# Temporaries of the next stage's right operands held once, and the first half's norm sums behind the third product, in a two-layer streaming encoder step

## The chip, the cores and the metric

The kernel runs on one core of one Trainium2 chip. The metric is the device time of one execution in microseconds. Engines are named as in the profile: PE (TensorE, the matrix products; PEld is its loading of weights), DVE (VectorE), ACT (ScalarE), POOL (GpSimd) and SP (SyncE, which issues most loads). L451 means line 451 of the kernel before. An order of instructions or a row of the profile that names a tile as `fr<-W` reads: tile fr is written from W.

## The reference

Two layers, each a mixer (gated linear attention, then latent attention) between two half-step SwiGLU feed-forward blocks, for 512 new frames, 32 frames of a running stream and 16 meta tokens, which makes T = 560 columns. All of it is float32. The change is in the feed-forward blocks (FFN):

```python
def rmsnorm(x, w):
    x32 = x.astype(jnp.float32)
    y = x32 * lax.rsqrt(jnp.mean(x32 * x32, axis=-1, keepdims=True) + RMS_EPS)
    return (y * w.astype(jnp.float32)).astype(x.dtype)

def swiglu_half(h, norm_w, w_gate, w_up, w_down):
    hn = rmsnorm(h, norm_w)
    return h + 0.5 * ((jax.nn.silu(hn @ w_gate) * (hn @ w_up)) @ w_down)
...
    for i in range(DEPTH):
        hp = swiglu_half(hp, ffn1_norm[i], ffn1_w_gate[i], ffn1_w_up[i], ffn1_w_down[i])
...
        hp = swiglu_half(hp, ffn2_norm[i], ffn2_w_gate[i], ffn2_w_up[i], ffn2_w_down[i])
```

The model width is 1024, the width of the FFN 2816. The same weights serve both groups of frames.

## The kernel before

**Precision.** Each float32 operand is split into a high part (an ACT cast, L331) and a low part (a DVE subtraction, L332). A product is three matmuls per 128 rows: high by high (L378), low weight by high (L379), high weight by low (L381). Of weights the two parts are called whi and wlo, of activations ah and al, and of right operands both are x.

**Gate and up products.** Both are computed by Strassen's scheme: seven products of quadrants in place of eight, each of 24 matmuls with 272 or 280 columns, into the PSUM tiles A, B and C. For each pair of 128-row tiles of the FFN, `gate_up` runs through them in this order, named by their right operands: b11 (into A), b21 (C), t6 (A), t5 (B), t7 (A), t4 (C), b22 (B). `quads` supplies the left operands: it loads the quadrants r11, r12, r21 and r22 of the weights into tiles fr (256 KB a load, two loads a quadrant, six tiles in turn) and forms four sums on DVE (L451), s1 = r21 + r22, r21 + r11, r11 + s1 and r12 + r11. The sum r11 + s1 is the left operand of t6, s1 that of t5, r21 + r11 that of t7. Each is then cast and split. The first two left operands of an FFN are loaded and cast ahead of it (`first_weights`).

**Right operands.** For all FFNs but the first, the right operands of the seven products are made while the stage before still runs: whenever its last loop has finished a piece of the stream h (one of eight row tiles m, one of two column halves hf), `Quads.__call__` makes the parts for it. Its temporaries b12, t5, q (four 280-column parts) and sq2 (the squares for the norm) come from the pool xt. The first FFN makes its right operands itself (`lazy`).

**Norm.** The norm's scale is applied to the results of the products and not to their operands. `Net.roots` makes it for one column half: PE adds the squares over the rows (L410, three matmuls of one column), DVE takes the inverse root in 11 small operations (L424 to L432), PE spreads it over the rows (L417, three transposes), and ACT copies it (L272). `finish` then combines the products (L497, L499), multiplies by the scale (L501), applies SiLU and the product of gate and up (L504), and splits the result into ah and al.

**Stages.** ffn(1,0) = f1_0, the first mixer, ffn(2,0) = f2_0, ffn(1,1) = f1_1, the second mixer, ffn(2,1) = f2_1. The row tiles of the FFN are handled in five groups; the down products of a group (tiles Y, weights raw, one load of 512 KB a row tile) fill gaps between products of the next group, and those of the last group form a loop of 16 pieces, in whose course the next stage's right operands are made. Where f2_0 and f2_1 begin, that loop is the mixer's output product (tiles ps), of 16 pieces too.

**Order.** The program is written stage by stage; the compiler's scheduler then sets the order on each engine by its own model of readiness. Each engine and each queue works strictly in its order. Loads go through SP's queue. A tile of a pool is an address in SBUF; a write to it waits until the last reader of whatever lay at that address is done, also if that was a tile of another pool. In f2_0 and f1_1 the pool xt lies, in the kernel before, at 148704 to 166624 bytes of each partition, and overlaps the end of the six fr tiles (125056 to 149632); in f2_1 it lies at 151936 to 169856, and its second q overlaps the first fr tile (168928 to 173024).

Of the kernel before, what the change touches and what calls it, by code (L numbers as in the profile page):

```python
# [10 lines left out]
F32 = mybir.dt.float32  # L11
# [7 lines left out]
P = 128  # L19
# [3 lines left out]
T = SEQ + LS + META  # L23
# [72 lines left out]
class Normed(list):  # L96
# [7 lines left out]
    def parts(self, m, hf):  # L104
        net, nc = self.net, self.net.nc
        c = slice(*self.halves[hf])
        if not self:
            self.extend((net.xtile(), net.xtile()) for _ in range(ND))
            self.y = net.np_.tile([P, T], F32, name="yn", tag="yn")
        hm, w = net.h[:, m, c], net.nv[:, self.w0 + m:self.w0 + m + 1]  # L110
        hi, lo = self[m]
        nc.scalar.activation(hi[:, c], hm, AF.Copy, scale=w)
        nc.vector.scalar_tensor_tensor(lo[:, c], hm, w, hi[:, c].bitcast(F32), op0=ALU.mult, op1=ALU.subtract)

    def square(self, hf):
        c0, c1 = self.halves[hf]
        m = self.squared[hf]
        self.net.square(self.net.h[:, m, c0:c1], c1 - c0, hf, m == 0)
        self.squared[hf] += 1
# [15 lines left out]
class Quads(Normed):  # L135
# [51 lines left out]
    def parts(self, m, hf):  # L187
        net, nc, n = self.net, self.net.nc, self.n
        v = nc.vector
        i = m % 4  # L190
        if hf == 0:
            self.scaled_parts("b11" if m < 4 else "b21", i, m)
        elif m < 4:
            b12, t5 = (self.tmp.tile([P, 280], F32, name=x, tag=x, bufs=2)[:, :n] for x in ("b12", "t5"))
            nc.scalar.activation(b12, self.piece(m, 1), AF.Copy, scale=self.weight(m))
            v.scalar_tensor_tensor(t5, self.piece(m, 0), self.weight(m), b12, op0=ALU.mult, op1=ALU.subtract)
            net.split(*self.place("t5", i), t5)
            self.kept[i] = b12, t5
        else:
            b12, t5 = self.kept.pop(i)  # L200
            q = self.tmp.tile([P, 4, 280], F32, name="q", tag="q", bufs=2)
            t6, b22, t7, t4 = (q[:, j, :n] for j in range(4))
            nc.scalar.activation(b22, self.piece(m, 1), AF.Copy, scale=self.weight(m))
            v.scalar_tensor_tensor(t6, t5, -1.0, b22, op0=ALU.mult, op1=ALU.subtract)
            v.tensor_tensor(t7, b22, b12, op=ALU.subtract)
            v.scalar_tensor_tensor(t4, self.piece(m, 0), self.weight(m), t6, op0=ALU.mult, op1=ALU.add)
            self.place("t6", i)
            t = self.sets["t6"][1][i]
            net.split(t[:, 0, :, :n], t[:, 1, :, :n], q[:, :, :n])

    def square(self, m):

        net, nc = self.net, self.net.nc
        c1 = self.halves[1][1]
        sq = self.tmp.tile([P, T], F32, name="sq2", tag="sq2", bufs=2)
        nc.scalar.activation(sq[:, :c1], net.h[:, m, :c1], AF.Square)
        for hf, (a, b) in enumerate(self.halves):
            if m == 0:
                net.accs[hf] = net.np_.tile([P, 280], F32, name="acc", tag="acc")
                nc.vector.tensor_copy(net.accs[hf][:, :b - a], sq[:, a:b])  # L220
            else:
                acc = net.accs[hf][:, :b - a]
                nc.vector.tensor_tensor(acc, acc, sq[:, a:b], op=ALU.add)
# [66 lines left out]
class Net:  # L290
# [176 lines left out]
    def gate_up(self, i, l, f, xs, act, raws, tp, between):  # L467


        nc = self.nc  # L470
        v = nc.vector
        n = xs.n
        left = self.quads(i, l, f, raws, xs.early, xs.left)
        done = []

        def product(to, op, more=False):
            if xs.lazy and op in ("b11", "b21"):
                w, x = next(left), xs.operand(op)
            else:
                x, w = xs.operand(op), next(left)  # L480
            for j in range(2):
                self.mm(to[:, j, :n], w, 4 * j, x, (0, n), more)

        def gap():
            done.append(0)
            between(len(done))

        def copy(of, tag):
            r = tp.tile([P, 2, 280], F32, name="r", tag=tag, bufs=1)
            nc.scalar.copy(r[:, :, :n], of[:, :, :n])  # L490
            return r

        def finish(j, hf, bank, r, how):
            gu = tp.tile([P, 2, 280], F32, name="gu", tag="gu", bufs=2)
            b, r, t = bank[:, :, :n], r[:, :, :n], gu[:, :, :n]
            if how == "neg":
                v.scalar_tensor_tensor(t, b, -1.0, r, op0=ALU.mult, op1=ALU.subtract)  # L497
            else:
                v.tensor_tensor(t, b, r, op=how)  # L499
            y = xs.scale(hf).unsqueeze(1).to_broadcast([P, 2, n])  # L500
            v.tensor_tensor(t, t, y, op=ALU.mult)  # L501
            g, u = gu[:, 0, :n], gu[:, 1, :n]
            nc.scalar.activation(g, g, AF.Silu)
            v.tensor_tensor(g, g, u, op=ALU.mult)  # L504
            c = slice(*xs.halves[hf])
            self.split(act[j][0][:, c], act[j][1][:, c], g)

        first = not xs.finish
        A = self.bank2("A")
        product(A, "b11")  # L510
        r1 = copy(A, "ra")
        gap()
        C = self.bank2("C")
        product(C, "b21")
        if not first:
            finish(0, 0, C, r1, ALU.add)
        gap()
        if first and not xs.lazy:
            xs.roots(0)
        product(A, "t6", True)  # L520
        r2 = copy(A, "rb")
        gap()
        if first and xs.lazy:
            xs.roots(0)
        B = self.bank2("B")
        product(B, "t5")
        p5 = copy(B, "rc")
        if first:
            finish(0, 0, C, r1, ALU.add)
            xs.roots(1)  # L530
        gap()
        product(A, "t7", True)
        r3 = copy(A, "ra")
        finish(1, 1, A, p5, "neg")
        gap()
        D = self.bank2("C")
        product(D, "t4")
        finish(1, 0, D, r3, ALU.subtract)
        gap()
        product(B, "b22", True)  # L540
        finish(0, 1, B, r2, ALU.add)
        gap()
# [373 lines left out]
    def softmax(self, pool, p, parts):  # L916

        nc = self.nc
        st = pool.tile([P, 8], F32, name="st", tag="st", bufs=4)
        for i, (s, n, c) in enumerate(parts):  # L920
            nc.vector.reduce_max(st[:, i:i + 1], s[:, :n], axis=AX.X)
        if len(parts) == 2:
            nc.vector.tensor_tensor(st[:, 0:1], st[:, 0:1], st[:, 1:2], op=ALU.max)
        nc.vector.tensor_scalar(st[:, 2:3], st[:, 0:1], -SCALE, None, op0=ALU.mult)
        for i, (s, n, c) in enumerate(parts):
            nc.scalar.activation(p[:, c:c + n], s[:, :n], AF.Exp, bias=st[:, 2:3], scale=SCALE,
                                 accum_out=st[:, 3 + i:4 + i])
        if len(parts) == 2:
            nc.vector.tensor_tensor(st[:, 3:4], st[:, 3:4], st[:, 4:5], op=ALU.add)
        nc.vector.reciprocal(st[:, 5:6], st[:, 3:4])  # L930
        n = sum(q[1] for q in parts)
        nc.vector.tensor_scalar(p[:, :n], p[:, :n], st[:, 5:6], None, op0=ALU.mult)
# [637 lines left out]
```

## Time and profile before

| | |
|---|---|
| median of 3 runs | 2114.17 us (2113.75 to 2114.99) |
| the profiled execution | 2109.41 us, of which 2107.5 are its span |
| mean granted clock of TensorE | 0.982 |
| PE busy | 2026.0 us, 96% of the span |
| DVE busy | 1643.2 us, 78% |
| ACT busy | 1018.4 us, 48% |
| POOL busy | 51.4 us, 2% |
| loads from HBM | 176.84 MB, 86 GB/s over the span |

The profile records one execution. The busy share of an engine is an average over all stages. A row of the timeline has the start in us, the duration in us, the engine, the line, the operation with its output and inputs, a count and, in brackets, how long the engine stood idle ahead of it and which operation ended that. The chain that ended last is followed back from the last instruction, at each step to what released it. The clock is what the throttle granted TensorE, 1.00 being full speed.

### The profile page before, as it was taken

What the parts mean: (1) busy time and instruction counts of PE and PEld (TensorE: products, weight loads), DVE (VectorE), ACT (ScalarE), POOL (GpSimd) and SP (SyncE); (2) the same over time, 40 slices, a digit from 0 to 9 for tenths busy, and PEclk for the clock granted to TensorE, in tenths of its full rate; (3) what the DMA queues carried; (4) which work ended last, traced back from release to release, by engine and by line L of the source; (5) the groups of instructions that cost most, each with busy time, mean ns of one, the idle gap of its engine ahead of it and who ended that gap; (6) DMA issues with size and microseconds to landing.
All of it is one profiled execution on the core that took longest, in us unless ns stands there. A gap on an engine that the chain in (4) does not pass through costs nothing.

```text
span 2107.5 us, 38039 instructions
## 1 busy us (share of the span) xinstructions
PE 2026.0 (96%) x15290; PEld 1980.2 (94%) x15290; DVE 1643.2 (78%) x3097; ACT 1018.4 (48%) x1822; POOL 51.4 (2%) x117
## 2 busy tenths in 40 slices
PE   5999999999999899999989999999999979999997
PEld 5999999989999799999979999999988969999997
DVE  8887878556658888788778877886788788878884
ACT  6444445455445444445545444454575454444451
POOL 0000000101110000000000000000210000000000
PEclk8999999999999899999989999999999989999998
DMA  3323222222221332322222322222211223232221
GB/s 131 106 87 107 93 96 78 77 68 71 73 80 55 108 103 82 106 86 91 81 95 96 105 92 91 95 83 92 61 51 59 71 86 100 90 111 91 96 72 62
DMA packets 93633, 183.29 MB, mean 87 GB/s; under 512 B 10433, under 2 KB 22081, under 8 KB 93457
## 3 DMA queue, kind: packets, MB, share of 16 engines
q1 hardware_dynamic: 89632, 176.24, 26.1%
q10 hardware_dynamic: 3824, 4.63, 0.7%
q8 instruction: 120, 1.97, 0.4%
q14 instruction: 57, 0.46, 0.1%
HBM read 176.84 MB, written 3.99 MB: 86 GB/s over the span
## 4 chain that ended last, share of the span: by engine, by line
PE 82%; DVE 10%; ACT 3%; DMA 2%; issue 2%; SPq 0%; POOL 0%; DVEq 0%; ACTq 0%; POOLq 0%
PE Y L381 8%; PE Y L378 8%; PE Y L379 8%; PE A L379 5%; PE A L381 5%; PE A L378 5%; PE ps L378 4%; PE ps L381 4%; PE ps L379 4%; PE B L378 3%; PE B L379 3%; PE B L381 3%; PE C L379 3%; PE C L381 3%; PE C L378 3%; DVE wlo L332 3%
## 5 line engine op out<-in xcount | busy, mean ns | idle before, releaser
L332 DVE TENSOR_TENSOR wlo<-fr,whi 128x1024 fp32r<-128x1024 f32 x302 | 363.9, 1216 | 17.2 <-ACT whi L331 17.0
L378 PE MATMUL Y<-ah,whi 128*128 128x280 f32 (+1 forms) x1408 | 373.8, 291 | 1.9 <-ACT ah L331 1.0
L379 PE MATMUL Y<-ah,wlo 128*128 128x280 f32 (+1 forms) x1408 | 373.4, 292 | 0.0
L331 ACT CAST whi<-fr 128x1024 fp32r<-128x1024 f32 x302 | 313.3, 1049 | 92.9 <-PE C L381 34.6
L378 PE MATMUL A<-x,whi 128*128 128x280 f32 (+1 forms) x1056 | 286.3, 296 | 29.5 <-ACT whi L331 29.5
L379 PE MATMUL A<-x,wlo 128*128 128x280 f32 (+1 forms) x1056 | 285.7, 296 | 1.0 <-DVE wlo L332 1.0
L378 PEld LDWEIGHTS Y<-ah,whi 128*128 128x128 f32 x1408 | 265.2, 188 | 3.4 <-ACT ah L331 1.7
L556 DVE SCALAR_TENSOR_TENSOR h<-Y,h 128x280 f32<-128x280 f32 (+1 forms) x320 | 140.9, 443 | 161.9 <-PE Y L381 161.2
L379 PEld LDWEIGHTS Y<-ah,wlo 128*128 128x128 f32 x1408 | 265.4, 188 | 0.0
L332 DVE TENSOR_TENSOR wlo<-raw,whi 128x512 fp32r<-128x512 f32 (+5 forms) x237 | 203.6, 861 | 76.7 <-ACT whi L331 71.9
L331 ACT CAST whi<-raw 128x512 fp32r<-128x512 f32 (+5 forms) x237 | 176.0, 744 | 173.4 <-PE ps L381 55.2
L381 PE MATMUL Y<-al,whi 128*128 128x280 f32 (+1 forms) x1408 | 233.9, 292 | 0.0
L378 PEld LDWEIGHTS A<-x,whi 128*128 128x128 f32 x1056 | 203.9, 193 | 31.1 <-ACT whi L331 31.1
L451 DVE TENSOR_TENSOR fr<-fr 128x1024 f32<-128x1024 f32 x176 | 214.5, 1219 | 20.4 <-DMA fr<-W 18.1
L379 PEld LDWEIGHTS A<-x,wlo 128*128 128x128 f32 x1056 | 203.7, 193 | 1.7 <-DVE wlo L332 1.4
L381 PEld LDWEIGHTS Y<-al,whi 128*128 128x128 f32 x1408 | 201.2, 189 | 0.0
L378 PE MATMUL B<-x,whi 128*128 128x280 f32 (+1 forms) x704 | 188.6, 293 | 3.4 <-ACT whi L331 3.4
L379 PE MATMUL C<-x,wlo 128*128 128x280 f32 (+1 forms) x704 | 187.1, 292 | 3.5 <-DVE wlo L332 3.5
L379 PE MATMUL B<-x,wlo 128*128 128x280 f32 (+1 forms) x704 | 187.4, 292 | 0.8 <-DVE wlo L332 0.8
L378 PE MATMUL C<-x,whi 128*128 128x280 f32 (+1 forms) x704 | 187.4, 291 | 0.6 <-ACT whi L331 0.6
L381 PE MATMUL A<-x,whi 128*128 128x280 f32 (+1 forms) x1056 | 181.2, 294 | 0.0
L490 ACT COPY r<-A 128x560 f32<-128x560 f32 (+1 forms) x132 | 82.2, 623 | 174.1 <-PE A L381 173.8
(368 smaller groups left out, 4059.2 us busy)
## 6 DMA issues: line engine op xcount, KB each, us to landing
fr<-W SPq DMA_DIRECT2D x352, 256.0 KB, 3.4
raw<-W SPq DMA_DIRECT2D x80, 512.0 KB, 3.5
raw<-W SPq DMA_DIRECT2D x112, 256.0 KB, 2.9
raw<-W SPq DMA_DIRECT2D x40, 128.0 KB, 2.1
h<-xT SPq DMA_DIRECT2D x3, 560.0 KB, 7.6
raw<-W SPq DMA_DIRECT2D x4, 384.0 KB, 3.1
o_y<-h SPq DMA_DIRECT2D x8, 136.0 KB, 2.2
o_y<-h ACTq DMA_DIRECT2D x8, 136.0 KB, 1.9
```

The costliest lines, as they stand in the source:

```text
L331: self.nc.scalar.copy(hi, src)
L332: self.nc.vector.tensor_tensor(lo, src, hi.bitcast(F32), op=ALU.subtract)
L378: f(hi[:, b0 + k, :], xh[:, c], start=not more and k == 0, stop=False)
L379: f(lo[:, b0 + k, :], xh[:, c], start=False, stop=False)
L381: f(hi[:, b0 + k, :], xl[:, c], start=False, stop=k == n - 1)
L451: add = lambda out, x, y: nc.vector.tensor_tensor(out, x, y, op=ALU.add)
L490: nc.scalar.copy(r[:, :, :n], of[:, :, :n])
L556: nc.vector.scalar_tensor_tensor(self.h[:, m, c], Y[:, :n], 0.5, self.h[:, m, c], op0=ALU.mult, op1=ALU.add)
```

## The change

The temporaries b12, t5, q and sq2 are held in one buffer each in place of two, which makes the pool xt 8960 bytes a partition in place of 17920. With it its address moves: to 157664 to 166624 in f2_0 and f1_1 (over the second gu tile only), and to 151936 to 160896 in f2_1 (its q now over the tile ra, the copy of the first product, and no fr tile). And `gate_up` asks for the first half's norm sums behind the third product (t6) for every FFN, which only the lazy first one did.

```diff
--- before.py
+++ after.py
@@ -191,14 +191,14 @@
         if hf == 0:
             self.scaled_parts("b11" if m < 4 else "b21", i, m)
         elif m < 4:
-            b12, t5 = (self.tmp.tile([P, 280], F32, name=x, tag=x, bufs=2)[:, :n] for x in ("b12", "t5"))
+            b12, t5 = (self.tmp.tile([P, 280], F32, name=x, tag=x, bufs=1)[:, :n] for x in ("b12", "t5"))
             nc.scalar.activation(b12, self.piece(m, 1), AF.Copy, scale=self.weight(m))
             v.scalar_tensor_tensor(t5, self.piece(m, 0), self.weight(m), b12, op0=ALU.mult, op1=ALU.subtract)
             net.split(*self.place("t5", i), t5)
             self.kept[i] = b12, t5
         else:
             b12, t5 = self.kept.pop(i)
-            q = self.tmp.tile([P, 4, 280], F32, name="q", tag="q", bufs=2)
+            q = self.tmp.tile([P, 4, 280], F32, name="q", tag="q", bufs=1)
             t6, b22, t7, t4 = (q[:, j, :n] for j in range(4))
             nc.scalar.activation(b22, self.piece(m, 1), AF.Copy, scale=self.weight(m))
             v.scalar_tensor_tensor(t6, t5, -1.0, b22, op0=ALU.mult, op1=ALU.subtract)
@@ -212,7 +212,7 @@
 
         net, nc = self.net, self.net.nc
         c1 = self.halves[1][1]
-        sq = self.tmp.tile([P, T], F32, name="sq2", tag="sq2", bufs=2)
+        sq = self.tmp.tile([P, T], F32, name="sq2", tag="sq2", bufs=1)
         nc.scalar.activation(sq[:, :c1], net.h[:, m, :c1], AF.Square)
         for hf, (a, b) in enumerate(self.halves):
             if m == 0:
@@ -515,12 +515,10 @@
         if not first:
             finish(0, 0, C, r1, ALU.add)
         gap()
-        if first and not xs.lazy:
-            xs.roots(0)
         product(A, "t6", True)
         r2 = copy(A, "rb")
         gap()
-        if first and xs.lazy:
+        if first:
             xs.roots(0)
         B = self.bank2("B")
         product(B, "t5")
```

What stands in a row on the engines follows from the scheduler. PE at the start of f2_0, before (C is the second product, A the third, t6, and B the fourth, t5; ry is the inverse root):

```order
L381 MATMUL C_8011<-x_7603,whi_7780 128x280
L381 MATMUL C_8011<-x_7604,whi_7780 128x280
L410 MATMUL Y_8036<-ones_67,acc_7660 128x1 x3
L417 MATMUL Y_8127<-ident_66,ry_8040 128x128 x3
L410 MATMUL Y_8137<-ones_67,acc_7662 128x1 x3
L417 MATMUL Y_8187<-ident_66,ry_8141 128x128 x3
L378 MATMUL A_7978<-x_7609,whi_8064 128x280
L378 MATMUL B_8094<-x_7605,whi_8095 128x280
L379 MATMUL A_7978<-x_7609,wlo_8065 128x280
L378 MATMUL A_7978<-x_7610,whi_8064 128x280
```

The same place after:

```order
L381 MATMUL C_8011<-x_7603,whi_7780 128x280
L381 MATMUL C_8011<-x_7604,whi_7780 128x280
L410 MATMUL Y_8076<-ones_67,acc_7660 128x1 x3
L378 MATMUL A_7978<-x_7609,whi_8046 128x280
L378 MATMUL B_8094<-x_7605,whi_8095 128x280
L379 MATMUL A_7978<-x_7609,wlo_8047 128x280
L378 MATMUL A_7978<-x_7610,whi_8046 128x280
L379 MATMUL A_7978<-x_7610,wlo_8047 128x280
```

and 40 rows on, at the end of B:

```order
L381 MATMUL B_8094<-x_7607,whi_8095 128x280
L381 MATMUL B_8094<-x_7608,whi_8095 128x280
L417 MATMUL Y_8127<-ident_66,ry_8080 128x128 x3
L410 MATMUL Y_8137<-ones_67,acc_7662 128x1 x3
L378 MATMUL A_7978<-x_7609,whi_8155 128x280
L379 MATMUL A_7978<-x_7609,wlo_8156 128x280
L378 MATMUL A_7978<-x_7610,whi_8155 128x280
```

The sums of the first half (L410) stay ahead of A; the transposes (L417) and the second half's sums move behind B. f2_1 is alike; in f1_1 the fourth product, B, begins ahead of the third.

DVE at the start of f2_0, before, the end of the second chain of roots and the four sums of quadrants:

```order
L504 TENSOR_TENSOR gu_8125<-gu_8125 128x280
L431 TENSOR_TENSOR rt_8143<-rt_8143,rv_8142 128x3
L432 SCALAR_TENSOR_TENSOR ry_8141<-rt_8143,ry_8141 128x3
L430 TENSOR_TENSOR rt_8143<-ry_8141 128x3
L431 TENSOR_TENSOR rt_8143<-rt_8143,rv_8142 128x3
L332 TENSOR_TENSOR al0_7975<-gu_8125,ah0_7974 128x280
L432 SCALAR_TENSOR_TENSOR ry_8141<-rt_8143,ry_8141 128x3
L451 TENSOR_TENSOR fr_8060<-fr_8054,fr_8057 128x1024
L451 TENSOR_TENSOR fr_8054<-fr_8054,fr_7979 128x1024
L451 TENSOR_TENSOR fr_7979<-fr_7979,fr_8060 128x1024
L451 TENSOR_TENSOR fr_7982<-fr_7982,fr_7979 128x1024
L332 TENSOR_TENSOR wlo_8065<-fr_7979,whi_8064 128x1024
```

and after:

```order
L499 TENSOR_TENSOR gu_8125<-C_8011,r_8009 128x560
L451 TENSOR_TENSOR fr_8042<-fr_8036,fr_8039 128x1024
L424 TENSOR_SCALAR rv_8081<-Y_8076 128x3
L451 TENSOR_TENSOR fr_8036<-fr_8036,fr_7979 128x1024
L425 TENSOR_SCALAR ry_8080<-rv_8081 128x3
L451 TENSOR_TENSOR fr_7979<-fr_7979,fr_8042 128x1024
L430 TENSOR_TENSOR rt_8082<-ry_8080 128x3
L451 TENSOR_TENSOR fr_7982<-fr_7982,fr_7979 128x1024
L332 TENSOR_TENSOR wlo_8047<-fr_7979,whi_8046 128x1024
L431 TENSOR_TENSOR rt_8082<-rt_8082,rv_8081 128x3
L332 TENSOR_TENSOR wlo_8096<-fr_8042,whi_8095 128x1024
L432 SCALAR_TENSOR_TENSOR ry_8080<-rt_8082,ry_8080 128x3
```

The four sums now follow the first result (L499) directly, and the small operations of the roots stand between sums and casts. f2_1 is alike.

SP in the last down loop of f2_0, ahead of f1_1 (raw_11996 to raw_12326 are down weights and the first two left operands; fr_12449 to fr_12748 belong to f1_1), before:

```order
L358 DMA fr_11654<-W 128x512 x2
L341 DMA raw_11996<-W 128x1024
L341 DMA raw_12030<-W 128x1024
L341 DMA raw_12137<-W 128x1024
L341 DMA raw_12171<-W 128x1024
L358 DMA raw_12278<-W 128x512 x2
L358 DMA raw_12285<-W 128x512 x2
L341 DMA raw_12292<-W 128x1024
L341 DMA raw_12326<-W 128x1024
L341 DMA raw_12820<-W 128x256
L341 DMA raw_12882<-W 128x256
```

and after:

```order
L358 DMA fr_11654<-W 128x512 x2
L358 DMA fr_12449<-W 128x512 x2
L358 DMA fr_12452<-W 128x512 x2
L341 DMA raw_11996<-W 128x1024
L358 DMA fr_12506<-W 128x512 x2
L358 DMA fr_12509<-W 128x512
L341 DMA raw_12030<-W 128x1024
L358 DMA fr_12509<-W 128x512
L341 DMA raw_12137<-W 128x1024
L358 DMA fr_12748<-W 128x512 x2
L341 DMA raw_12171<-W 128x1024
L358 DMA raw_12278<-W 128x512 x2
```

The first ten loads of f1_1's quadrants moved from behind the last of the down weights to between them; the casts of its third and fourth left operands moved into the end of this loop too. In f2_1 the place of the loads on SP is the same, directly behind raw_20697; what they wait for is not: before, the first of them waits for the reader of the second q, and after only for tiles of the mixer. In f2_0 they stand where they stood, and wait for the mixer's last output product as before.

## Prediction

> **What bounds the kernel now.** I read the page first: busy shares, the chain that ended last, then the costliest groups with the idle time before them.
>
> ```profile
> span 2107.5 us, 38039 instructions
> ...
> PE 82%; DVE 10%; ACT 3%; DMA 2%; issue 2%; SPq 0%; POOL 0%; DVEq 0%; ACTq 0%; POOLq 0%
> ...
> L378 PE MATMUL A<-x,whi 128*128 128x280 f32 (+1 forms) x1056 | 286.3, 296 | 29.5 <-ACT whi L331 29.5
> ...
> L490 ACT COPY r<-A 128x560 f32<-128x560 f32 (+1 forms) x132 | 82.2, 623 | 174.1 <-PE A L381 173.8
> ```
>
> The kernel is bound by PE, so time is only to be had where PE stands still. The largest single wait is in the third row: product A waits for a cast weight, 29.5 us in all. At the three starts that the diff touches it is 3.76, 3.76 and 6.17 in the rows below, 13.7 of the 29.5. (The last row is used further down.) I then read those three starts in the timeline, PE alone. Stage f2_0 (start, length, what, idle time before it and releaser):
>
> ```profile
> 685.12 0.72 PE L410 MATMUL Y<-ones,acc 128*128 128x1 f32 x6
> ...
> 693.59 0.87 PE L417 MATMUL Y<-ident,ry 128*128 128x128 f32 x3 [3.30 <-DVE ry L432]
> 698.23 0.60 PE L378 MATMUL A<-x,whi 128*128 128x280 f32 x1 [3.76 <-ACT whi L331]
> 699.18 0.60 PE L378 MATMUL B<-x,whi 128*128 128x280 f32 x1 [0.35 <-ACT whi L331]
> 699.58 0.57 PE L379 MATMUL A<-x,wlo 128*128 128x280 f32 x1
> ...
> 707.05 0.29 PE L378 MATMUL A<-x,whi 128*128 128x280 f32 x1
> 707.18 0.29 PE L379 MATMUL A<-x,wlo 128*128 128x280 f32 x1
> ```
>
> The second product (C) ends where L410 begins, at 685.1; the fifth (t7) begins at 707.05. Between them lie two products of 24 matmuls, which at full clock start 0.13 us apart (the last two rows; 0.129 over a product, 3.1 us). So 21.9 us are spent on 6.2 us of products. What ends the idle time is the chain of waits, same stage:
>
> ```profile
> 685.90 0.73 DVE gu L499
> ...
> 693.45 1.15 DVE fr L451
> 694.61 1.24 DVE fr L451
> 695.87 1.24 DVE fr L451
> 697.24 0.84 issue
> 698.08 1.05 ACT whi L331
> ```
>
> DVE's sums of weight quadrants (L451) begin only after both root chains, because they stand behind them on DVE; from the first sum (693.4) to the first A is 4.8 us, and to the second matmul of A (699.58) 6.1. What else could hold the sums is their data. Loads in 682 to 692 us, and the rate at which the DMA engines moved them:
>
> ```profile
> fr<-W SPq DMA_DIRECT2D x4, 256.0 KB, 6.3
> ```
>
> ```profile
> 685.00:688.00 3.00, 0.85 (x9) 0.76 (x7) 2.76 (x10) 0.16 (x1) 0.00 (x0) 1.00 1.02 374
> ```
>
> 256 KB at 374 GB/s are 0.70 us, and loads queue. The last half of quadrant r22, issued near 682.3, lands at about 688.6.
>
> **The change, part by part.** It adds and takes away no arithmetic: the same sums, casts, products and loads, in another order and other buffers.
>
> *f2_0.* The loads still wait for the last matmul of the mixer's output (same buffers' owner), so they land when they did. The order now has L410 of the first half, then A and B, and DVE's four sums ahead of the root chain. The first sum starts at 688.7 (landing; L499 has ended by 686.6), 4.7 us before 693.4; first A at 693.5, its second matmul at 694.8, and 0.3 later for the small root operations that now stand between the sums: 695.1. Off that gain come the clock and the roots. Busy time in windows of 3.41 us, where the eighth column is the granted clock (columns: length, then busy us and count of PE, PEld, DVE, ACT, POOL, then clock, DMA share, GB/s):
>
> ```profile
> 685.79:689.20 3.41, 0.53 (x6) 0.47 (x5) 2.53 (x13) 0.00 (x0) 0.00 (x0) 1.00 0.89 341
> 689.20:692.61 3.41, 1.09 (x7) 1.01 (x5) 2.10 (x10) 1.05 (x3) 0.00 (x0) 0.50 0.00 2
> ...
> 699.44:702.85 3.41, 3.41 (x15) 3.33 (x16) 3.41 (x4) 1.58 (x2) 0.00 (x0) 0.50 0.59 181
> 702.85:706.26 3.41, 3.41 (x28) 3.41 (x27) 0.41 (x2) 1.57 (x2) 0.00 (x0) 1.00 0.85 274
> ```
>
> After a window with little PE work the clock is 0.50, and it is back one window after a full one; a full window holds 15 matmuls at half clock (0.23 us each), so half clock costs 0.10 us a matmul. PE still has nothing to do from 685.9 to 693.5, so the drop stays. If the windows keep their phase, matmuls run slowly from 695.1 to 699.44, 19 matmuls in place of 14: 0.5 us more. The 46 matmuls left after the opening end at 699.44 + 27 x 0.129 = 703.0. Then the first half's L417 x3 and the second half's L410 x3, which used to run in idle time, now stand in PE's stream (about 0.4 + 0.36 from their spacing): t7 begins at 703.8 in place of 707.05, 3.25 us earlier. The second L417 x3 (0.4) now stands inside the next block's first product, and waits for a chain of 11 small DVE operations which stand between casts; I allow 0.5 for that. Net 2.3; ends 0 (sums no earlier than L499 plus a full chain, phase unlucky: +1.5) and 3.5 (no wait, lucky phase). I take 2.2.
>
> [...]
>
> *f1_1.* This is where most of it lies. Here the new, smaller temporaries leave the weight buffers untouched (only the second gu buffer is overlapped), and the order moves the weight loads, the four sums and the casts into the last down phase of the FFN before.
>
> ```profile
> 1077.00 0.72 PE L410 MATMUL Y<-ones,acc 128*128 128x1 f32 x6
> ...
> 1089.12 0.60 PE L378 MATMUL A<-x,whi 128*128 128x280 f32 x1 [3.76 <-ACT whi L331]
> ...
> 1098.68 0.29 PE L378 MATMUL A<-x,whi 128*128 128x280 f32 x1
> ```
>
> Before: 21.7 us from the end of C to t7. After: B starts right behind L410, with its weights cast. L410 x3 (0.36), 48 matmuls (6.2), L417 x3 and L410 x3 (0.76): 7.3 us, t7 at 1084.3, 14.4 earlier. PE has no idle window left there, so I count no half clock (what it cost is contained in the 21.7). Off come 0.4 for the second L417 and 0.5 for waits on the roots: 13.5.
>
> The price is paid 60 us earlier. On SP two pairs of fr loads now go out ahead of the down weight raw_11996, three loads ahead of raw_12030, one ahead of raw_12137, and a pair ahead of raw_12171. What the first of these down weights feeds, on SP, ACT and PE:
>
> ```profile
> 1014.29 10.14 SPq L341 DMA_DIRECT2D raw<-W  x4
> ```
>
> ```profile
> 1017.96 1.05 ACT L331 CAST whi<-raw 128x1024 fp32r<-128x1024 f32 x1 [0.70 <-DMA raw<-W]
> ```
>
> ```profile
> 1023.12 0.40 PE L378 MATMUL Y<-ah,whi 128*128 128x280 f32 x1 [0.27 <-ACT ah L331]
> ```
>
> The cast already waits 0.70 us for its load, and behind it in ACT's order stand the casts of ah for which PE waits at 1023.12. Four loads ahead are at most 4 x 0.70 = 2.8 us, less what has landed before raw_11996's own issue (they go out 0.47 us apart from about 1012.5); three more ahead of the next are 2.1. Delay of the ah cast: 0.5 to 3.5, where the upper end is 2.8 and a third of the second; all of it reaches PE. I take 2.0, nearer the upper end since both casts stand in that chain. In the rest of this phase DVE gets 4.9 us of sums and ACT four casts early. ACT waited there for the pieces themselves:
>
> ```profile
> 1068.36 0.53 ACT L195 ACTIVATE b<-h,nv 128x280 f32<-128x280 f32 x1 [2.48 <-DVE h L556]
> ```
>
> With such gaps at two of every four pieces, they fit. Net 11.5; low end 13.5 - 3.5 - 1.5 (a clock window dropped to half) - 1.5 (roots late) = 7, high end 14.4.
>
> *f2_1.* The second q buffer overlapped r11's load buffer, so SP's loads waited for DVE's last right operand. With one q it doesn't.
>
> ```profile
> 1712.32 1.29 DVE L332 TENSOR_TENSOR x<-q,x 128x1088 fp32r<-128x1088 f32 x1 [0.52 <-ACT x L331]
> ...
> 1723.48 5.00 DVE L451 TENSOR_TENSOR fr<-fr 128x1024 f32<-128x1024 f32 x4
> ```
>
> ```profile
> 1697.76 0.33 SPq L341 DMA_DIRECT2D raw<-W  x1
> ```
>
> ```profile
> 1713.68 4.67 SPq L358 DMA_DIRECT2D fr<-W  x10
> ```
>
> ```profile
> 1716.60:1733.70 17.10, 7.76 (x32) 6.92 (x33) 12.55 (x22) 6.69 (x9) 0.00 (x0) 0.50 0.53 164
> ```
>
> ```profile
> 1712.66 0.72 PE L410 MATMUL Y<-ones,acc 128*128 128x1 f32 x6
> ...
> 1728.36 0.59 PE L378 MATMUL A<-x,whi 128*128 128x272 f32 x1 [6.17 <-ACT whi L331]
> ...
> 1729.70 0.57 PE L379 MATMUL A<-x,wlo 128*128 128x272 f32 x1
> ...
> 1737.34 0.29 PE L378 MATMUL A<-x,whi 128*128 128x272 f32 x1
> ```
>
> The loads now go out behind raw, near 1698, and with ten at 0.70 us have landed by 1710. The one q lies over the copy ra, which therefore waits for the same DVE operation (1713.6, then 0.62 of copy by the page's L490 row), L499 follows at 1714.3, and the first sum at 1715.0 in place of 1723.5. With the 6.1 + 0.3 us of f2_0 from first sum to A's second matmul: 1721.4, 8.3 earlier. The clock drops at 1716.6 (before: until 1733.7, five windows); after two idle ones it comes back at 1726.9, or at 1723.5 if the partly filled one counts. So, worked as in f2_0, t7 lies between 1728.9 and 1730.4 with the roots counted, 7 to 8.4 earlier; less 0.4 for the second L417 and 0.5 for its wait: 6.1 to 7.5. I take 6.0, below them, as this stage has an extra SP and ACT step in front; ends 4 and 8.
>
> *One buffer for sq2, b12, t5 and q.* ACT may write a temporary only when DVE has read the last one. Each is used once every two pieces; the row at 1068.36 shows ACT idle 2.48 us before such a piece. I cost it at nothing, bounded by 0 and 0.3 us a stage. If that cover went, PE would wait at every piece (rival below). POOL has nothing moved.
>
> **Sum.** 2.2 + 11.5 + 6.0 = 19.7 us. The profiled execution took 2109.41 us (2107.5 of span and 1.9 around it); 2109.4 - 19.7 = 2089.7. The median of the three runs, 2114.17, lies 4.76 above the profiled one, so **2094.5 us**. Differences under 0.2% (4.2 us) a measurement of this kernel could hardly tell from none.
>
> **Rivals.**
> 1. *The gain is eaten by the order.* DVE does sums, casts and the small root operations in one line; at the start of a stage it no longer gets ahead while PE idles, and the second half's scale comes later. For: DVE is busy most of each window above. Against: in the two windows where the clock drops it also had gaps. At the low ends, 0 + 7 + 4 = 11: 2103.
> 2. *More than forecast.* The loads collide with nothing, no root is waited for: 3.5 + 14.4 + 8 = 25.9: 2088.
> 3. *No change.* The sums start no earlier, because what frees the buffers is another owner than the temporaries, or because PE's L410 and L417 keep their place. For: in f2_0 the loads do keep their time, and L410 stays ahead. Against: 1713.68 follows the end of DVE's x<-q (1713.61) by 0.07, so that wait was the binding one. Then about 2114.
> 4. *Slower.* One mechanism: single temporaries put ACT and DVE in turn in the 48 pieces of three output loops, and PE waits at each. Above 19.7 / 48 = 0.41 us a piece the gain is gone, above 0.50 it is slower by more than 0.2%. A whole cast in turn, 0.8 us a piece, gives 2133. Against: ACT's 2.48 us of idle time per piece.
>
> **How the numbers follow.** Forecast 0.56, rival 1 0.24, rival 2 0.09, rival 3 0.07, rival 4 0.04. Faster by over 0.2% are the forecast and rivals 1 and 2: 0.89; same 0.07; slower 0.04. The forecast's own range is 2091 to 2099, from the ends of the largest term. The range for 8 in 10 takes in most of rival 1 and rival 2: 2087 to 2105.
>
> **What would show it.** The waits: product A's wait for whi at L378 falls from 29.5 us by 10 or more, L417's wait for ry almost goes. f2_0: first L451 sum directly after L499, t7 about 3 us earlier, still some 0.50 clock. f1_1: fr loads near 1012 on SP, no 0.50 window at its start, PE idle of 1 to 3 us about 1020 for ah. f2_1: fr loads near 1698 and the first sum 1.5 us after x<-q ends. Wrong it would be if PE shows new waits for ah or h at many pieces (rival 4), or if A still waits 3 us at f1_1.

## The result: 0.9% faster, 2095.07 us against a forecast of 2094.5

The changed kernel takes 2095.07 us in the median of 4 runs (2091.03 to 2098.88), the kernel before 2114.58 in the median of 4 (2113.75 to 2117.99): 0.9905 of it, 95% interval 0.9887 to 0.9922. The profiled execution's span went from 2107.5 to 2089.2 us. A later set of runs gave 0.9918 (0.9900 to 0.9936). Two later executions, one of the changed kernel (3279 us at a mean clock of 0.556) and one of a further kernel (2185 us at 0.857), ran in a slow state and stand in no median and no ratio below. The forecast time came out within 1 us. One of its terms, one of the signs to look for, and the account of what the change owes its effect to did not come out.

The page after, its span, the chain that ended last and the group that stood third before:

```profile
span 2089.2 us, 38053 instructions
...
PE 86%; DVE 7%; ACT 2%; DMA 2%; issue 2%; SPq 0%; POOL 0%; DVEq 0%; ACTq 0%; POOLq 0%
...
L378 PE MATMUL A<-x,whi 128*128 128x280 f32 (+1 forms) x1056 | 285.6, 295 | 29.6 <-ACT whi L331 29.6
```

PE's share of the chain grew by 4 points, DVE's fell by 3: DVE work left the path. But the wait of A stayed at 29.6. The waits of the whole execution, after (in all, how often, longest), show which fell instead:

```profile
PE A L378 <- ACT whi L331: 29.6, 5, 8.5
...
PE Y L378 <- ACT ah L331: 4.9, 3, 2.9
...
PE Y L417 <- DVE ry L432: 4.1, 3, 2.2
```

and before:

```profile
PE A L378 <- ACT whi L331: 29.5, 6, 8.8
PE Y L417 <- DVE ry L432: 21.4, 8, 3.3
...
PE Y L378 <- ACT ah L331: 1.0, 3, 0.4
```

Of 50.9 us that A and L417 waited before, 33.7 are left; a new wait of 3.9 us for ah stands against them. At f2_0, PE's timeline after (L417's waits are gone, and A carries one long wait in place of three):

```profile
686.64 0.72 PE L410 MATMUL Y<-ones,acc 128*128 128x1 f32 x6
695.07 0.60 PE L378 MATMUL A<-x,whi 128*128 128x280 f32 x1 [7.71 <-ACT whi L331]
...
705.04 0.37 PE L378 MATMUL A<-x,whi 128*128 128x280 f32 x1
```

From the end of C to t7 it is now 18.4 us in place of 21.9. DVE there:

```profile
687.42 0.73 DVE L499 TENSOR_TENSOR gu<-C,r 128x560 f32<-128x560 f32 x1
690.20 1.22 DVE L451 TENSOR_TENSOR fr<-fr 128x1024 f32<-128x1024 f32 x1 [2.04 <-DMA fr<-W]
```

The first sum stands directly behind L499 and waits for the load, as forecast. f1_1 after, from the end of C to t7:

```profile
1079.45 0.72 PE L410 MATMUL Y<-ones,acc 128*128 128x1 f32 x6
1080.04 0.38 PE L378 MATMUL B<-x,whi 128*128 128x280 f32 x1
...
1087.18 0.37 PE L378 MATMUL A<-x,whi 128*128 128x280 f32 x1
```

7.7 us in place of 21.7, with no wait at all. f2_1 after, on SP, DVE and PE:

```profile
1686.17 0.33 SPq L341 DMA_DIRECT2D raw<-W  x1
1686.55 5.47 SPq L358 DMA_DIRECT2D fr<-W  x10
```

```profile
1702.17 1.29 DVE L332 TENSOR_TENSOR x<-q,x 128x1088 fp32r<-128x1088 f32 x1 [0.52 <-ACT x L331]
1704.20 0.72 DVE L499 TENSOR_TENSOR gu<-C,r 128x544 f32<-128x544 f32 x1 [0.73 <-ACT r L490]
1704.84 1.21 DVE L451 TENSOR_TENSOR fr<-fr 128x1024 f32<-128x1024 f32 x1
```

```profile
1702.58 0.72 PE L410 MATMUL Y<-ones,acc 128*128 128x1 f32 x6
1709.70 0.59 PE L378 MATMUL A<-x,whi 128*128 128x272 f32 x1 [6.40 <-ACT whi L331]
...
1711.04 0.57 PE L379 MATMUL A<-x,wlo 128*128 128x272 f32 x1
...
1719.14 0.37 PE L378 MATMUL A<-x,whi 128*128 128x272 f32 x1
```

From the end of C to t7 it is 16.6 us in place of 24.7. The loads leave directly behind raw, and the first sum starts 1.4 us after x<-q has ended. And the price, in the down loop ahead of it, on SP, ACT and PE:

```profile
1010.24 1.76 SPq L358 DMA_DIRECT2D fr<-W  x4
1012.54 0.33 SPq L341 DMA_DIRECT2D raw<-W  x1
```

```profile
1019.15 1.05 ACT L331 CAST whi<-raw 128x1024 fp32r<-128x1024 f32 x1 [3.64 <-DMA raw<-W]
```

```profile
1024.31 0.47 PE L378 MATMUL Y<-ah,whi 128*128 128x280 f32 x1 [2.95 <-ACT ah L331]
```

```profile
1024.10:1027.50 3.40, 3.19 (x14) 3.19 (x15) 3.40 (x7) 0.99 (x3) 0.00 (x0) 0.56 0.46 177
```

The down weight left SP no later than before (1012.54, with everything at this place 1.75 us earlier than before's 1014.29), but its data came behind four fr loads: the cast began 6.6 us after issue in place of 3.7. The cast waits 3.64, ah comes late, PE pauses 2.95 us, and the last row shows a window of half clock behind the pause.

**Counting by steps.** All kernels but the one with extra matmuls issue the same 15290 PE instructions; in that one the extra ones are left out of the count. For each I take the start of the n-th in the trace of before less that of the n-th here; a step is by how much this difference grows across a place (us, positive is time won; places by the time in the trace of before):

| place | forecast | after | after_again | b12_once | once_16992 | roots_only | once_17024 |
|---|---|---|---|---|---|---|---|
| f2_0, 660 to 725 | 2.2 | 2.95 | 0.75 | 2.49 | 2.27 | -1.40 | -1.39 |
| of it, from the end of C on | 2.2 | 2.95 | 2.31 | 2.47 | 2.27 | -1.40 | -1.40 |
| down loop, 1000 to 1045 | -2.0 | -4.20 | -5.10 | -4.11 | -3.75 | 0.19 | -1.33 |
| f1_1, 1045 to 1135 | 13.5 | 13.57 | 13.57 | 13.57 | 13.57 | -0.52 | -0.18 |
| f2_1, 1690 to 1760 | 6.0 | 5.35 | 5.17 | 6.21 | 6.11 | -1.42 | -1.69 |
| of it, from the end of C on | 6.0 | 6.86 | 6.68 | 7.73 | 7.63 | 0.10 | -0.17 |
| all other places | 0 | 0.59 | -5.10 | -2.25 | 2.09 | -2.33 | 0.48 |

The last two kernels have the order of before on every engine, so their steps show how far two executions differ by themselves: up to 1.7 us at a place, 0.5 and 2.3 over the rest.

Two of the places begin in the mixer, ahead of what the change touches. There a window of half clock that the execution of before does not have costs 1.5 us (0.75 against 2.31, 5.35 against 6.86 in the table): near 675 us in after_again alone, and ahead of f2_1 in all six kernels of the table, so also in the two that have the order of before. The same stretch ahead of f2_1 in before and after:

```profile
1698.70:1701.70 3.00, 3.00 (x26) 3.00 (x25) 2.62 (x8) 1.77 (x4) 0.00 (x0) 1.00 0.18 49
```

```profile
1687.00:1690.00 3.00, 3.00 (x16) 3.00 (x15) 1.83 (x5) 0.88 (x3) 0.00 (x0) 0.50 0.78 238
```

What the change does to the two stages is therefore read from the end of C on. In f2_0 the two kernels with the order of before lose 1.40 us there, because their half clock lasts one window longer than before's (0.50 from 689.9 to 707.0 in roots_only, from 689.2 to 702.85 in before). Against those two the gain of f2_0 would be 3.7 to 4.4 us.

### The profile page after: what moved, and what is told of

The parts are those of the page before. It is cut to its first block, busy times and chain, and to the rows that moved or that the text cites. A ratio compares the mean times of both kernels' runs of the same rounds, so it can differ in the third digit from the quotient of the medians.

```text
span 2089.2 us, 38053 instructions
## 1 busy us (share of the span) xinstructions
PE 2022.0 (97%) x15290; PEld 1977.7 (95%) x15290; DVE 1638.2 (78%) x3097; ACT 1018.8 (49%) x1822; POOL 51.7 (2%) x117
## 4 chain that ended last, share of the span: by engine, by line
PE 86%; DVE 7%; ACT 2%; DMA 2%; issue 2%; SPq 0%; POOL 0%; DVEq 0%; ACTq 0%; POOLq 0%
PE Y L381 8%; PE Y L378 8%; PE Y L379 8%; PE A L379 6%; PE A L381 6%; PE A L378 6%; PE ps L378 4%; PE B L379 4%; PE B L378 4%; PE B L381 4%; PE ps L381 4%; PE ps L379 4%; PE C L379 4%; PE C L381 4%; PE C L378 4%; DVE wlo L332 2%
## 5 line engine op out<-in xcount | busy, mean ns | idle before, releaser
L378 PE MATMUL A<-x,whi 128*128 128x280 f32 (+1 forms) x1056 | 285.6, 295 | 29.6 <-ACT whi L331 29.6
L381 PE MATMUL Y<-al,whi 128*128 128x280 f32 (+1 forms) x1408 | 233.9, 292 | 0.0
L451 DVE TENSOR_TENSOR fr<-fr 128x1024 f32<-128x1024 f32 x176 | 214.4, 1218 | 19.7 <-DMA fr<-W 17.8
L381 PEld LDWEIGHTS Y<-al,whi 128*128 128x128 f32 x1408 | 201.2, 189 | 0.1
L381 PE MATMUL A<-x,whi 128*128 128x280 f32 (+1 forms) x1056 | 181.0, 294 | 0.0
```

Of the source, the lines that this page charges most:

```text
L378: f(hi[:, b0 + k, :], xh[:, c], start=not more and k == 0, stop=False)
L381: f(hi[:, b0 + k, :], xl[:, c], start=False, stop=k == n - 1)
L451: add = lambda out, x, y: nc.vector.tensor_tensor(out, x, y, op=ALU.add)
```

## The experiments: is it the room, the single buffers, or the place of the norm sums?

The prediction took the new order as given and did not ask which of the two edits makes it. Building each alone answers for the order: with the norm sums moved alone, all engines have exactly the order of before; with b12 alone held once, PE and SP have exactly that of the change. The old temporaries took 17920 bytes and lay 928 bytes over the weight tiles. Theory ROOM: clearing that overlap is the whole change. Rivals: ROOTS (the move of the norm sums) and BUFFERS (what is saved, or what single buffers cost).

**roots_only**: only the norm sums are moved.

```diff
-        if first and not xs.lazy:
-            xs.roots(0)
         product(A, "t6", True)
...
-        if first and xs.lazy:
+        if first:
             xs.roots(0)
```

> Only the first half's norm sums are asked for behind the third product; all temporaries keep two buffers. The built order on every engine is then that of the kernel before. Theory ROOM (what moves the work is the 928 bytes by which the old temporaries lay over the weight tiles, and with them the scheduler's order): no change, 2114 within 4 us, no step at any of the three stage starts. Rival ROOTS (moving the norm sums frees DVE and PE at the starts): about half of the 18.5 us, 2105, with steps of about 3 us at f2_0 and 6 at f1_1.

Measured: 2115.74 against 2116.07 us of before, 1.000 (0.9987 to 1.0013). ROOTS falls: alone, the second edit does nothing that can be measured.

**b12_once**: only b12 is held once; all else as before.

```diff
-            b12, t5 = (self.tmp.tile([P, 280], F32, name=x, tag=x, bufs=2)[:, :n] for x in ("b12", "t5"))
+            b12, t5 = (self.tmp.tile([P, 280], F32, name=x, tag=x, bufs=1 if x == "b12" else 2)[:, :n] for x in ("b12", "t5"))
```

> Only the temporary b12 is held once (1120 bytes less, 16800 in place of 17920); t5, q and sq2 keep two buffers and the norm sums keep their place in the program. Theory ROOM: 1120 bytes are enough to clear the 928 bytes of overlap, PE's order is that of the changed kernel, and so is the time: 2095 within 4 us, with the steps of the changed kernel: +3.3 us at f2_0, -4.2 in the down loop ahead of f1_1, +14.0 at its start, +5.5 at f2_1. Rival ROOTS: 2105 to 2114. Rival BUFFERS (the gain grows with what is saved): about an eighth of 8960 bytes, 2112.

Measured: 2093.46 us, 0.9903 (0.9878 to 0.9927), with all four steps of the change. One tile of 1120 bytes brings the whole effect.

**once_17024** and **once_16992**: all temporaries once, as in the change, but with unused columns on sq2.

```diff
-        sq = self.tmp.tile([P, T], F32, name="sq2", tag="sq2", bufs=1)
+        sq = self.tmp.tile([P, T + 2016], F32, name="sq2", tag="sq2", bufs=1)
```

That is the kernel with 17024 bytes; the other has 2008 in place of 2016.

> The changed kernel with sq2 made wider by unused columns, so that all temporaries are held once but take 17024 bytes, 32 more than fit beside the weight tiles. The built order is that of the kernel before. Theory ROOM: 2114 within 4 us, and no step at any stage. It also prices the single buffers by themselves, since nothing else differs from before: within 1 us by my forecast (0 to 0.3 a stage); the rival that single temporaries put ACT and DVE in turn would give up to 0.4 us in each of 48 pieces, 2120 or more.

> As the kernel with 17024 bytes, but 32 bytes less, which just fits. Theory ROOM: 2095 within 4 us, the steps of the changed kernel (+3.3, -4.2, +14.0, +5.5). Rival BUFFERS: no difference between the two sizes.

Measured: 2115.21 us, 1.0001 (0.9987 to 1.0014), and 2095.99 us, 0.9910 (0.9883 to 0.9936). Thirty-two bytes decide over 19 us. The first kernel differs from before in the single buffers alone, so these cost nothing within 0.14%: rival 4 of the prediction and BUFFERS fall together. PE at f1_1 in once_17024 has before's waits again:

```profile
1082.61 0.54 PE L417 MATMUL Y<-ident,ry 128*128 128x128 f32 x3 [2.38 <-DVE ry L432]
...
1087.02 0.87 PE L417 MATMUL Y<-ident,ry 128*128 128x128 f32 x3 [3.30 <-DVE ry L432]
1091.66 0.60 PE L378 MATMUL A<-x,whi 128*128 128x280 f32 x1 [3.77 <-ACT whi L331]
```

**hold_m6** and **hold_m1**: what the early loads cost. The change, and the first fr loads of f1_1 are issued behind the down weight of row tile 6 or 1.

```diff
+            with self.tc.issue_after(self.hold.ins) if (i, l) == (1, 1) and f < 4 else ExitStack():
-            self.quadrant(t, i, l, f, q)
+                self.quadrant(t, i, l, f, q)
```

Here `self.hold` is the load of that down weight. 

> The changed kernel with one edge more in the order: the first ten fr loads of f1_1 are issued behind the down weight of row tile 6 (raw_12171), not between the earlier ones. Theory COLLISION (the -4.2 us in the down loop ahead of f1_1 come from the four fr loads in front of raw_11996, through the casts in ACT's order, with half clock after the pause): the step there goes to 0 within 0.7, the pause of 2.95 us for ah at 1024 to below 0.5, and f1_1's start keeps its +13.6; time 4.2 less than the changed kernel, 2091. Rival CASTS (the early sums and casts of f1_1 fill ACT and DVE in that loop): the step stays between -2 and -4.

> The same, but the fr loads are held behind raw_11996 only, so three of them stand ahead of raw_12030 and one ahead of raw_12137. Theory COLLISION: the cast of raw_11996 no longer waits over 1 us for its load, that of raw_12030 does, by up to 3 x 0.70 = 2.1 us; the step in this loop lies between -0.3 and -2.5. Rival CASTS: -4 as before.

Measured: hold_m6 2088.91 us, 0.9881 (0.9856 to 0.9906); hold_m1 one run, 2095.16. f1_1's step stays 13.57 in both. The step in the down loop is -1.31 with hold_m6 and -0.87 with hold_m1. Two further kernels below keep hold_m6's order of loads there; over five executions of that order (hold_m6, hold_again, hold_late, hold_warm, warm_again) the steps are -1.31, -1.71, 0.03, 0.23 and 0.02, mean -0.55, against -4.2 (after), -5.1, -4.1 and -3.75 with the loads in front. COLLISION stands and CASTS falls, since the early casts are there in all of them. The forecast of "within 0.7" missed in two of the five, and so did that of a pause below 0.5 us (1.55 in hold_m6, 1.98 in hold_again): there the load took long with nothing in front of it. SP and ACT in hold_m6:

```profile
1016.28 0.33 SPq L341 DMA_DIRECT2D raw<-W  x1
```

```profile
1021.12 1.05 ACT L331 CAST whi<-raw 128x1024 fp32r<-128x1024 f32 x1 [1.97 <-DMA raw<-W]
```

and in hold_late, the same order here:

```profile
1016.49 0.33 SPq L341 DMA_DIRECT2D raw<-W  x1
```

```profile
1020.05 1.05 ACT L331 CAST whi<-raw 128x1024 fp32r<-128x1024 f32 x1 [0.67 <-DMA raw<-W]
```

From issue to cast it is 4.84 and 3.56 us. The DMA packets of the traces show what else ran there. In hold_m6 a packet of 16 KB on queue q8, of the kind "instruction", ran from 1018.88 to 1019.85 us, in the middle of the load. Fifteen of the 16 packets of 4 bytes that close the load had ended by 1019.34, the last only at 1020.61. hold_again has the same picture (15 by 1020.50, the last at 1021.71). In hold_late the q8 packet began at 1019.50, just before the load ended at 1019.56, and in hold_warm and warm_again none ran during it. So in both executions with the long load one of its sixteen ends came 1.2 to 1.3 us behind the others, and such a packet had fallen into its middle. That the packet is the cause is argued from these five executions; no run moved it by itself. In hold_m1 the first cast waited 1.14 us for its load, a little more than its expectation allowed. The next waited 0.44 us, where over 1 us was expected, so the three loads ahead of it cost less than forecast.

**hold_warm**: does the clock cost what the steps assume? hold_m6, and idle PE time filled.

```diff
+            for _ in range(34 if l == 0 else 28):
+                self.tc.keep_in_program_order(nc.tensor.matmul(B[:, 0, :P], self.ident, self.ident, start=True, stop=True))
         product(A, "t6", True)
```

> The kernel hold_m6, and in f2_0 and f2_1, between the norm sums of the first half and the third product, 34 and 28 matmuls of the identity by itself into the bank of B, which the fourth product overwrites. They fill PE's pause of 7.7 and 6.4 us if one takes 0.2 us. Theory CLOCK (half clock after the pause costs about 0.1 us for each of about 20 matmuls in each of the two stages): no 0.50 window at their starts and 2 us less at each, 4 us below hold_m6. If one takes under 0.13 us they end early and the clock may still fall; if over 0.25 they delay A by 1 us or more and the gain is gone.

Measured: 2088.77 us, 0.9877 (0.9856 to 0.9898), the same as hold_m6 within its interval. The first profile shows no half clock from 689 to 705 and 1700 to 1715 (hold_warm), and PE in f2_0 waiting for the next thing (the added lines shift the line numbers: L380 is high by high, L381 low weight by high):

```profile
689.00:705.00 16.00, 14.90 (x123) 14.50 (x122) 12.96 (x22) 7.34 (x9) 0.00 (x0) 1.00 0.45 152
1700.00:1715.00 15.00, 14.40 (x118) 13.82 (x117) 12.49 (x22) 7.52 (x10) 0.00 (x0) 1.00 0.38 113
```

```profile
695.34 0.40 PE L380 MATMUL A<-x,whi 128*128 128x280 f32 x1 [0.17 <-ACT whi L331]
696.66 0.40 PE L381 MATMUL A<-x,wlo 128*128 128x280 f32 x1 [0.92 <-DVE wlo L332]
```

Steps 3.61 and 6.45 against hold_m6's 2.39 and 6.02: 1.7 us in place of the expected 4. In the second execution, against hold_again, the whole places show nothing (0.47 and 6.14 against 0.50 and 6.29). From the end of C on they show 0.0 in f2_0 (2.00 against 2.03), where a window of half clock stands from 702.8 to 706.2 in spite of the extra matmuls, and 1.4 in f2_1 (7.67 against 6.30). The clock term is at most half of what I expected.

**hold_late**: hold_m6, and the fourth sum behind the low part of A's left operand.

```diff
+        with self.tc.issue_after(low.ins) if i == 2 and f == 0 else ExitStack():
-        add(r12, r12, r11)
+            add(r12, r12, r11)
```

> The kernel hold_m6, and in f2_0 and f2_1 the fourth sum (r12 + r11, for the seventh product) is put behind the low part of the third product's left operand on DVE. By theory ORDER (DVE's order from the first sum to the second matmul of A is what bounds these starts) that matmul comes 1.2 us earlier in both stages, 2 us in all with half clock counted. Rival: the clock, which is tied to windows and not to the matmul, eats it: under 0.5 us.

Measured: 2091.49 us, 0.9893 (0.9872 to 0.9913), steps 2.25 and 6.19, no gain. DVE at f2_0 in hold_late shows why: with the fourth sum moved away (the rows are the third sum, which is L454 in this kernel, a root operation and the low part), the low part starts where it did:

```profile
696.03 1.23 DVE L454 TENSOR_TENSOR fr<-fr 128x1024 f32<-128x1024 f32 x1
...
698.34 0.16 DVE L432 TENSOR_TENSOR rt<-ry 128x3 f32<-128x3 f32 x1
698.42 1.22 DVE L332 TENSOR_TENSOR wlo<-fr,whi 128x1024 fp32r<-128x1024 f32 x1
```

In hold_m6 the third sum begins at 696.10 and the low part at 698.50: 2.4 us later in both. The low part needs ACT's cast of the third sum. The first matmul of A, which waits for the same cast, starts at 698.38 in hold_late, so the low part could not have begun earlier; the fourth sum ran beside that cast. ORDER was wrong in this point, and the rival, the clock, did not eat a gain either: there was none to eat.

**after_again**, **hold_again**, **warm_again**: the change and its two descendants on one chip.

> The changed kernel once more, beside the next two on the same chip. By its first runs 0.9905 of the kernel before.

> The kernel hold_m6 once more. Theory COLLISION: 3 to 4 us below the changed kernel of this call, and a step between -1.5 and +0.3 in the down loop ahead of f1_1, against -4 there.

> The kernel hold_warm once more. From the steps of its first profile (1.2 us at f2_0, 0.4 at f2_1) 1.6 us below hold_again; at 5 rounds that is about what can be told apart.

Measured: 2096.7, 2091.4 and 2091.43 us in the median; 0.9918 (0.9900 to 0.9936), 0.9896 (0.9876 to 0.9916) and 0.9888 (0.9867 to 0.9910) of before. Held loads lie 5.3 us below the change in the median, but the intervals overlap. The steps in the down loop (-0.55 in the mean of five against -4.3 in the mean of four) put 3 to 4 us on it, and I take these as real. The extra matmuls can't be told from none.

## Why the prediction was right, and where it wasn't

- *f2_0, 2.2.* Right in mechanism and, against the profiled execution of before, in size: from the end of C on 2.95, 2.31, 2.47 and 2.27. (The 0.75 of after_again holds 1.5 us of half clock in the mixer ahead.) The first sum waited for the load, and half clock stayed: 0.52 granted from 689.6 to 699.8, where the forecast, in the times of before, had it end at 699.44. That the size fits is partly luck, since before's own half clock there was a window shorter than in the other two executions of its order. The 1.5 us of an unlucky phase, in the low end, is close to what one window of half clock more cost at this place in those two, 1.40 us each.
- *f1_1's start, 13.5.* 13.57 in four executions. No half clock there: in after the granted clock is 1.00 from 1028 to 1100 us.
- *The price of the early loads, 2.0 with ends 0.5 and 3.5.* Mis-sized: 3.75 to 5.1, outside the ends. The pause was 2.95 us in after and 2.48 to 3.83 in the other three, about the 2.8 us that four loads at 0.70 make, where I had deducted what would land before. And I left the clock window out of the taken value: the pause itself, at 2.95 us, brought half clock for 3.4 us (1024.49 to 1027.90). The 1.5 for it stood only in the low end of f1_1.
- *f2_1, 6.0.* Right in mechanism, low in size: from the end of C on 6.86, 6.68, 7.73 and 7.63. Its working gave 6.1 to 7.5, and the 6.0 was taken below that for an extra SP and ACT step that the working already held. (Over the whole place it is 5.35, 5.17, 6.21 and 6.11, with the 1.5 us of half clock in the mixer.) Loads left SP at 1686.55, directly behind raw, and L499 did wait for the copy ra behind DVE's x<-q, as forecast.
- *One buffer each costs nothing.* Shown by once_17024, within 0.14%.
- *Sign to look for.* Wrong: A's wait did not fall by 10 us; it stayed at 29.6, and the time came out of L417's 21.4 us. A carries now what L417 used to wait first. A sum of idle time by releaser is not a sum of what can be won.
- *Cause.* The prediction priced the new order without saying that the move of the norm sums has no part in it. The order of before and after hangs on an overlap of 928 bytes, and f2_0, where the loads keep their time, gained only because the scheduler thereby ordered DVE and PE anew. How the scheduler gets from the overlap to the order, no run shows.
- *The total.* Between the two profiled executions the trace has 18.25 us, forecast were 19.7: the price took 2.2 more and the half clock ahead of f2_1 1.5, while f2_1 gave 0.9, f2_0 0.75 and the other places 0.6 more. So the sum came close because errors to both sides cancelled in part. That the median lay within 1 us of the forecast is partly luck too, since executions of this kernel lie up to 4 us to either side.

## What to carry to other kernels

Before pricing an edit, build each of its parts alone and compare the order: here one of two edits changed not a single row of the order, and 32 bytes in the size of a pool decided 19 us. When a prefetch becomes possible earlier, look for the load that it gets in front of, not only for the one that it serves; then hold it behind that load. Two waits in a row on one engine, for two producers, are one wait: taking the first away makes the second longer unless the second producer starts earlier too (in f2_0 A's wait grew from 3.76 to 7.71 us when L417's went). And a gain is read from the place where the order first differs, against more than one execution of the kernel before: 1.5 us of half clock ahead of a stage looked like a smaller gain of the stage.

## What the runs showed of the hardware

Executions of kernels with the same order differ by 5 us either way (before: 2109.16 to 2119.5 us in one set), partly through windows of half clock at places where another execution has none. The same 3.2 us of the second mixer in roots_only and before:

```profile
1526.30:1529.50 3.20, 3.20 (x12) 2.39 (x10) 0.98 (x5) 2.40 (x8) 0.00 (x0) 0.50 0.46 128
```

```profile
1523.60:1526.80 3.20, 3.20 (x22) 2.75 (x21) 2.30 (x13) 2.31 (x8) 0.00 (x0) 1.00 0.44 125
```

12 matmuls in place of 22; across this place roots_only lost 1.5 us. In the traces of before and after the granted clock changes 17 times each, and within one trace all changes lie whole multiples of 3.413 us apart, to within 0.02 us. So before has half clock from 689.20 to 702.85, 1081.73 to 1095.39 and 1716.61 to 1733.68 us, four, four and five times that length. In after the fall in f2_0 comes at 689.98 us, 0.78 later, which is no multiple of it: these two executions differ in phase. And a load of 512 KB with nothing in front of it took between 3.4 (hold_warm) and 4.9 us (hold_again) from issue to the cast that waited for it, 4.8 (hold_m6) and 4.9 in the two executions where a 16 KB instruction packet of 0.9 to 1.0 us ran in its middle.
